# Queue places of the operand splits in the output stages of a two-layer encoder: tied to weight copies and additions in place of matmuls

## The chip, the cores and the metric

One core of a Trainium2 chip runs the whole program once. The metric is the device time of one execution in microseconds, the median of several runs. An execution takes a little longer than the span that its profile shows: the profiled one took 1505.1 us with a span of 1503.3 us.

## The reference

Two layers over a sequence of 1024 tokens of width 1024, float32. Layer 0 has global attention, windowed attention and attention into 256 memory tokens; layer 1 has neighbourhood attention on a grid and again memory attention. In both the concatenated heads are gated and go through one output projection that is added to the residual stream:

```python
y = jnp.concatenate([ya, yb, ym], axis=-1) * jax.nn.silu(gate)   # 1536 wide
x = x + y @ w_out_even[e]
...
y = jnp.concatenate([yc, ym], axis=-1) * jax.nn.silu(gate)       # 1536 wide
x = x + y @ w_out_odd[o]
...
return rmsnorm(x, final_norm_gain)
```

The change touches only how these two output projections are ordered on the engines.

## The kernel before

**Split numbers.** A float32 number is fed to TensorE as two parts of a shorter type (float32r): a high part, which is the rounded copy, and a low part, which is the number less its high part. ScalarE (ACT) makes the copy (`copy`, L124), VectorE (DVE) or GpSimd (POOL) the subtraction. A product of two split numbers is three matmuls: high weight by high operand, high by low, low by high. `split` (L126) does this for an operand: the copy on ACT, the subtraction on DVE (L128). `w_parts` (L1263) does it for a weight unit of 128x384: the copy `wh` on ACT, the remainder `wl` (L1267) on DVE and POOL by turns (`either`). Both have four buffers, and so has the raw unit `wraw`, which SyncE's DMA queue (SP) loads at L1312.

**An output stage** (`out_project`, L1297; layer 0 at about 650 to 779 us of the span, layer 1 at about 1380 to 1503 us) multiplies 1024 x 1536 by 1536 x 1024 in halves, by a scheme of seven half-sized products in place of eight. In the order of the code these are y11, t1, t2, t3, y22, y21 and t4, named by their operands. The operands t1 to t4 are sums and differences of blocks of y that were made and stored earlier, as were the weight sums s1 to s4. Each product has four PSUM banks (output tiles of 128x512), and each bank takes two weight units (`u` = 0, 1) of three contraction tiles: 2 x 3 x 3 = 18 matmuls of 512 columns. For y11, t3, y22, y21 and t4 (`product`, L1315) a bank is finished before the next. For t1 and t2 (`products`, L1324) the first units of all four banks come first and then the second units. When a bank is done, `plus` (L1345) adds it on DVE into one or two of the result tiles c11, c22, c12, c21, into which the residual was loaded, and `square` makes their squares on ACT for the norm that follows.

**The operands** are loaded by `y_parts` (L1209), six tiles a product, one DMA each on SP (L1223), and split by `split` on ACT and DVE. Their buffers alternate. In layer 0, y11, y22 and t4 use the tags q, q, k, k, va (`va` holds two tiles), t1 and y21 use q, q, k, k, v (`v` holds two), t2 and t3 use six tiles each of H. In layer 1 t4 uses H as well, and c11 and c22 do too. y11 is stored ready split and is only loaded. So the transfer of y22's operand can start as soon as y11's matmuls have let go of its tiles, which is long before y22 runs, and y21's as soon as t1's have.

**What sets the order.** The program goes through a planner that runs a simulated clock. It gives every engine, and SP, a fixed list of instructions in the order in which they would become ready by that clock, and among ready ones by a priority, which is the place in the code, moved forward by a number that `ahead(kind)` gives (L35: in the first output stage weights by 300, in the second additions by 150). On the chip each engine then works through its list in order, and an instruction that waits for a semaphore holds up all behind it on that engine. `issue_after(ins)` is a limit for the planner: what is traced inside the block and runs on the engine of `ins` is listed behind `ins`; it adds no wait. `behind_held` (L1202) does that for the last copy and subtraction of the attention before (`held`), in layer 1; in layer 0 `held` is empty.

**The ties before.** In `products`, `ends[u, i]` keeps the last matmul of each bank. `y_parts` takes one matmul as `after` and puts the splits in an `issue_after` block of it: t3's splits behind the first bank of t1, y22's behind the last bank of t2, y21's behind t3, t4's behind y22 (L1384, L1393, L1403, L1419). t2's and t1's last three splits are put off (`later`) and traced one after each first unit of a bank (L1338 to L1340), behind `held` alone.

Of the kernel before, what the change touches and what calls it, by code (L numbers as in the profile page):

```python
# [64 lines left out]
class Trunk:  # L65
# [1133 lines left out]
        return tiles  # L1199

    @contextmanager
    def behind_held(self):  # L1202

        with ExitStack() as held:
            for i in self.held:
                held.enter_context(self.tc.issue_after(i.ins))
            yield

    def y_parts(self, yd, tags, kind, after=None):  # L1209

        nc = self.nc
        parts, later = [], deque()
        for k, t in enumerate(self.halves(tags, F32R)):
            hi, lo = t[:, 0, :], t[:, 1, :]
            raw = lo.bitcast(F32)
            y1, y2 = yd[k], yd[6 + k]
            with self.ahead("y"):
                if kind == "y11":
                    nc.sync.dma_start(t.bitcast(F32), y1[:, 2:4, :])
                    parts.append((lo, hi))  # L1220
                    continue
                src = dict(t1=y1[:, 1, :], t2=y2[:, 3, :], t3=y2[:, 2, :], y22=y2[:, 0, :], y21=y2[:, 1, :], t4=y2[:, 4, :])
                nc.sync.dma_start(raw, src[kind])  # L1223
                if kind in ("t1", "t2") and k > 2:
                    later.append((hi, lo, raw))
                else:
                    with self.behind_held(), self.tc.issue_after(after.ins) if after else nullcontext():
                        self.split(hi, lo, raw)
                parts.append((hi, lo))
        return (parts, later) if kind in ("t1", "t2") else parts  # L1230
# [32 lines left out]
    def w_parts(self, raw, engine, n=3):  # L1263
        h, l = (self.st(t, [128, UNIT, 128], F32R, pool=self.base, bufs=4)[:, :n] for t in ("wh", "wl"))
        hf, lf = (t.rearrange("p a b -> p (a b)") for t in (h, l))
        self.copy(hf, raw)
        engine.tensor_tensor(lf, raw, hf, op=OP.subtract)  # L1267
        return h, l

# [27 lines left out]
    def out_project(self, w, sd, yd, res, done, tags, banks, first, begun, last=False):  # L1297
# [4 lines left out]
        nc = self.nc  # L1302
        xb, yb = banks
        cut = [slice(u * 384, u * 384 + 384) for u in range(2)]

        def weights(i, kind, us=(0, 1)):

            src = sd[i][:, "3124".index(kind[1]), :] if kind[0] == "s" else w[i if kind[1] == "1" else 4 + i][:, 768 * (kind[2] == "2"):]
            for c in (cut[u] for u in us):
                with self.ahead("w"):  # L1310
                    raw = self.st("wraw", [128, UNIT * 128], pool=self.base, bufs=4)[:, :384]
                    nc.sync.dma_start(raw, src[:, c])  # L1312
                    yield self.w_parts(raw, self.either())

        def product(y, bank, ws, start, cols=slice(0, 512), ks=range(6)):  # L1315
            for u, (h, l) in enumerate(ws):
                for k in (k for k in range(3) if 3 * u + k in ks):
                    for e, (s, m) in enumerate(((h, 0), (h, 1), (l, 0))):
                        last = nc.tensor.matmul(bank, s[:, k, :], y[3 * u + k][m][:, cols],  # L1319
                                                start=start and u + k + e == 0, stop=u == 1 and k + e == 4,  # L1320
                                                skip_group_check=True)
            return last

        def products(y, banks, kind, start, ready=()):  # L1324
            ready = deque(ready)
            y, later = y
            ends.clear()
            for u in range(2):
                for i, bank in enumerate(banks):
                    (h, l), = (ready.popleft(),) if ready else weights(i, kind, (u,))  # L1330
                    for k in range(3):
                        for e, (s, m) in enumerate(((h, 0), (h, 1), (l, 0))):
                            end = nc.tensor.matmul(bank, s[:, k, :], y[3 * u + k][m], start=start and u + k + e == 0,
                                                   stop=u == 1 and k + e == 4, skip_group_check=True)
                    ends[u, i] = end
                    if u:
                        yield i
                    elif later:  # L1338
                        with self.behind_held(), self.ahead("y"):
                            self.split(*later.popleft())  # L1340

        def residual(x, nt, half):
            nc.sync.dma_start(x, res[nt][:, 512 * (2 - half):512 * (3 - half)])

        def plus(x, p, op=OP.add):  # L1345
            nc.vector.tensor_tensor(x, x, p, op=op)

        def square(x, k):

            sq = self.st("ph" if k else "vt", [128, 512])  # L1350
            nc.scalar.activation(sq, x, AF.Square)
            if 0 < k < 7:
                nc.gpsimd.tensor_tensor(sums[0], sums[0], sq, op=OP.add)
            else:
                sums.append(sq)
        ends = {}
        c11, c22, c12, c21 = (self.halves(t) for t in tags["c"])
        at = lambda c, i: c[i // 2][:, i % 2, :]

# [1 line left out]
        for i in range(4):  # L1361
            if i >= begun:
                with self.tc.issue_after(self.hold.ins) if self.hold else nullcontext():
                    product(first, xb[i], weights(i, "a11") if i > begun else self.early, True)
            residual(at(c11, i), i, 1)
            with self.behind_held(), self.ahead("sink"):
                plus(at(c11, i), xb[i])

        ready = [w for i in range(2) for w in weights(i, "s1", (0,))]
        y = self.y_parts(yd, tags["y"][1], "t1")  # L1370
        for i in products(y, yb, "s1", True, ready):
            residual(at(c22, i), 4 + i, 2)
            with self.ahead("sink"):
                plus(at(c22, i), yb[i])

        after = [ends[1, 0]]
        y = self.y_parts(yd, tags["y"][2], "t2")
        for i in products(y, xb, "s2", False):
            residual(at(c12, i), i, 2)
            with self.ahead("sink"):  # L1380
                plus(at(c12, i), xb[i])

        sums = []
        y = self.y_parts(yd, tags["y"][3], "t3", after[0])  # L1384
        for i in range(4):
            end = product(y, xb[i], weights(i, "s3"), False)
            residual(at(c21, i), 4 + i, 1)
            with self.ahead("sink"):
                plus(at(c22, i), xb[i])
                plus(at(c21, i), xb[i])  # L1390
                square(at(c22, i), i)

        y = self.y_parts(yd, tags["y"][4], "y22", ends[1, 3])  # L1393
        for i in range(4):
            ending = product(y, yb[i], weights(i, "s4"), False)
            with self.ahead("sink"):
                plus(at(c12, i), yb[i])
                square(at(c12, i), 4 + i)
# [1 line left out]
        next(norm)  # L1400

        sums = []
        y = self.y_parts(yd, tags["y"][5], "y21", end)  # L1403
        fence = None
        for i in range(4):
            parts = list(weights(i, "a12"))
            with self.tc.issue_after(fence.ins) if fence else nullcontext():
                end = product(y, xb[i], parts, True)
# [5 lines left out]
            with self.ahead("sink"):  # L1414
                x = at(c11, i)
                plus(x, xb[i])
                square(x, i)

        y = self.y_parts(yd, tags["y"][6], "t4", ending)  # L1419
        for i in range(4):  # L1420
            x = at(c21, i)
            if last and i == 3:
# [763 lines left out]
```

## Time and profile before

| | |
|---|---|
| median of 3 runs | 1505.27 us (1504.47 to 1507.01) |
| the profiled execution | 1505.1 us, span 1503.3 us |
| TensorE busy (PE) | 1473.3 us, 98% of the span |
| VectorE (DVE) | 1032.9 us, 69% |
| ScalarE (ACT) | 841.2 us, 56% |
| GpSimd (POOL) | 636.2 us, 42% |
| DMA, mean over the span | 181 GB/s |

How to read the lines of the profile: in a list of groups or of the timeline, `L124 ACT ACTIVATE wh<-wraw` is line 124 of the kernel, the engine, the operation, and the tile written from the tile read; buffer numbers are left out. The timeline gives the start, the length and in brackets the engine's idle time before the instruction with what ended it; `x2` after the shape means that two alike were merged. A row of waits gives the engine and line that waited, what released it, the sum in us, the count and the longest. A row of DMA issues gives the count and, below it, the least, median and greatest time from issue to landing in us. PEld is TensorE's weight load, which overlaps its matmuls.

### The profile page before, as it was taken

The page shows a single profiled execution, that of the slowest core. Times are in us where ns is not written, and L with a number is a line of the kernel's source. Part 1 is how long each engine was busy: PE and PEld are TensorE (multiplying, and loading weights), DVE is VectorE, ACT ScalarE, POOL GpSimd, SP SyncE. Part 2 cuts the span into 40 slices and gives each one's busy share as a digit, 9 for nine tenths or more (in the row PEclk, how much of TensorE's full clock was granted, in tenths as well). Part 3 has the DMA queues.
Part 4 walks back from the last instruction along what each step waited for, and adds up shares of the span by engine and source line. Part 5 has one row for each costly group of instructions (what it writes and reads, how often), then busy time and mean ns, then how long its engine had stood idle before and what let it go on. Part 6 is the DMA issues. An engine that isn't in the chain of part 4 may idle for free.

```text
span 1503.3 us, 25289 instructions
## 1 busy us (share of the span) xinstructions
PE 1473.3 (98%) x8377; PEld 1266.8 (84%) x8377; DVE 1032.9 (69%) x2122; ACT 841.2 (56%) x1855; POOL 636.2 (42%) x762
## 2 busy tenths in 40 slices
PE   9999999999999999998999999999999999999997
PEld 8898888989888788786879877888988888888786
DVE  6786777677676677667577766654447778788744
ACT  7743665655655456554445444444447777777442
POOL 1223668556665655533450000002225556754355
PEclk9999999999999999999999999999999999999999
DMA  8966344433444423388653434558675677688833
GB/s 282 323 157 178 111 121 165 126 125 118 129 126 136 133 89 129 120 272 268 197 174 117 139 135 148 151 157 284 200 262 154 209 231 223 218 285 312 284 111 138
DMA packets 173859, 271.90 MB, mean 181 GB/s; under 512 B 15648, under 2 KB 96800, under 8 KB 172704
## 3 DMA queue, kind: packets, MB, share of 16 engines
q1 hardware_dynamic: 173296, 270.20, 56.0%
q8 instruction: 66, 1.08, 0.3%
q14 instruction: 65, 0.53, 0.1%
q10 hardware_dynamic: 432, 0.09, 0.0%
HBM read 174.28 MB, written 83.89 MB: 172 GB/s over the span
## 4 chain that ended last, share of the span: by engine, by line
PE 78%; DVE 7%; DMA 7%; issue 3%; ACT 2%; POOL 1%; SPq 1%; POOLq 0%; DVEq 0%; ACTq 0%
PE pj L241 15%; PE pj L62 10%; PE x L1585 6%; PE tr L132 5%; PE pv L1055 4%; PE y L1585 4%; PE pv L62 3%; PE pj L1319 3%; PE s L62 3%; PE sa L1319 2%; PE pv L1585 2%; PE tr L62 2%; PE s L1319 2%; PE sa L1022 2%; PE sa L1023 2%
## 5 line engine op out<-in xcount | busy, mean ns | idle before, releaser
L124 ACT ACTIVATE ph<-tr 128x512 fp32r<-128x512 f32 (+2 forms) x336 | 180.9, 540 | 118.3 <-PE tr L132 76.9
L537 DVE TENSOR_TENSOR pl<-tr,ph 128x512 fp32r<-128x512 f32 (+2 forms) x336 | 205.5, 615 | 54.0 <-ACT ph L124 52.9
L241 PE MATMUL pj<-H,wh 128*128 128x512 f32 x704 | 234.6, 413 | 0.5 <-DVE vt L312 0.2
L157 POOL TENSOR_SCALAR wh<-wraw 128x512 fp32r<-128x512 f32 x48 | 34.4, 719 | 268.3 <-PE x L1585 234.9
L124 ACT ACTIVATE wh<-wraw 128x384 fp32r<-128x384 f32 (+1 forms) x163 | 89.1, 553 | 89.9 <-PE pj L1319 12.0
L241 PE MATMUL pj<-H,wl 128*128 128x512 f32 x352 | 139.1, 395 | 0.0
L241 PEld LDWEIGHTS pj<-H,wh 128*128 128x128 f32 x704 | 120.0, 189 | 18.7 <-POOL wh L157 0.6
L62 PE MATMUL pj<-H,wh 128*128 128x512 f32 x384 | 121.5, 397 | 0.0
L1108 POOL TENSOR_SCALAR pn<-pn,st 128x384 f32<-128x384 f32 (+1 forms) x128 | 75.3, 589 | 99.6 <-DVE st L1107 58.0
L132 PE MATMUL tr<-ident,P 128*128 128x128 f32 x752 | 115.7, 273 | 0.9 <-DVE pl L537 0.6
L1267 POOL TENSOR_TENSOR wl<-wraw,wh 128x384 fp32r<-128x384 f32 x56 | 61.9, 1107 | 117.8 <-ACT wh L124 101.1
L132 PEld LDWEIGHTS tr<-ident,P 128*128 128x128 f32 x752 | 88.9, 140 | 9.6 <-DVE pl L537 1.7
L1028 ACT ACTIVATE P<-sa,st 128x1024 f32<-128x1024 f32 x64 | 71.5, 1118 | 41.5 <-DVE st L1027 22.7
L1106 ACT ACTIVATE pn<-pn,st 128x384 f32<-128x384 f32 (+1 forms) x128 | 75.1, 587 | 35.0 <-DVE st L1103 32.6
L62 PE MATMUL s<-k,q 128*128 128x384 f32 (+1 forms) x352 | 86.5, 342 | 0.1
L1030 POOL TENSOR_SCALAR P<-P,st 128x1024 f32<-128x1024 f32 x64 | 73.9, 1158 | 29.0 <-DVE st L1029 26.9
L1027 DVE TENSOR_REDUCE st<-sa 128x1 f32<-128x1024 f32 x64 | 77.6, 1218 | 10.9 <-PE sa L1023 10.5
L241 PEld LDWEIGHTS pj<-H,wl 128*128 128x128 f32 x352 | 66.2, 188 | 15.1
L62 PE MATMUL pj<-H,wl 128*128 128x512 f32 x192 | 75.8, 395 | 0.0
L159 POOL TENSOR_TENSOR wl<-wraw,wh 128x512 fp32r<-128x512 f32 x52 | 68.2, 1315 | 9.5 <-ACT wh L124 6.9
L62 PEld LDWEIGHTS pj<-H,wh 128*128 128x128 f32 x384 | 66.6, 189 | 5.5
L840 PE MATMUL pj<-ah,H 128*128 128x256 f32 x384 | 70.5, 282 | 0.2
(558 smaller groups left out, 4172.3 us busy)
## 6 DMA issues: line engine op xcount, KB each, us to landing
wraw<-w_o SPq DMA_DIRECT2D x52, 256.0 KB, 3.7
y<-yb SPq DMA_DIRECT2D x24, 512.0 KB, 3.6
wraw<-s SPq DMA_DIRECT2D x64, 192.0 KB, 3.4
wraw<-w_e SPq DMA_DIRECT2D x44, 256.0 KB, 3.2
k<-k SPq DMA_DIRECT2D x42, 256.0 KB, 4.8
s<-bias SPq DMA_DIRECT2D x56, 192.0 KB, 2.0
y<-sg SPq DMA_DIRECT2D x20, 512.0 KB, 3.6
wq<-w_o SPq DMA_DIRECT2D x40, 256.0 KB, 3.3
```

The source lines that it names most:

```text
L62: return lambda *a, **k: self.tc.keep_in_program_order(getattr(self.engine, name)(*a, **k))
L124: return self.nc.scalar.activation(out, in_, AF.Copy, scale=scale)
L132: self.turned = self.fence = self.pe.transpose(o, i, self.ident)
L241: self.pe.matmul(a[:, :n], s[:, kt % UNIT, :], m, start=(kt == 0 and i == 0), stop=(kt == KT - 1 and i == 2))
L537: self.low = nc.vector.tensor_tensor(pl[:, :n], tr[:, :n], ph[:, :n], op=OP.subtract)
L1027: nc.vector.tensor_reduce(st[:, 0:1], s, axis=AX.X, op=OP.max, negate=True)
L1028: nc.scalar.activation(pt, s, AF.Exp, bias=st[:, 0:1], accum_out=st[:, 1:2])
L1030: self.normal = nc.gpsimd.tensor_scalar(pt, pt, st[:, 2:3], 0.5, op0=OP.mult, op1=OP.mult)
L1106: nc.scalar.activation(o, o, AF.Exp, bias=st[:, 0:1], scale=-1.0, accum_out=st[:, 2:3])
L1108: normal = nc.gpsimd.tensor_scalar(o, o, st[:, 3:4], 0.5, op0=OP.mult, op1=OP.mult)
L1319: last = nc.tensor.matmul(bank, s[:, k, :], y[3 * u + k][m][:, cols], start=start and u + k + e == 0, stop=u == 1 and k + e == 4, skip_gro ...
L1585: self.last = nc.tensor.matmul(bank, ws[s][:, k, :], b[k][m], start=start and k + i == 0, stop=k == UNIT - 1 and i == 2, skip_group_check= ...
```

## The change

The ties are made to instructions of the two engines on which the splits run. `w_parts` keeps the last weight copy on ACT (`self.high`), `plus` the last addition on DVE (`self.added`), and `behind_held` takes more instructions to stand behind. `after` becomes such a pair: for t3 the pair in the middle of t1's second half, for y22 that at the end of t2, for y21 that at the end of t3, for t4 that at the end of y22. The put-off splits of t1 and t2 are listed behind the last weight copy on ACT. `ends` and the matmuls kept in `end` and `ending` for this go. No instruction with work is added or removed, and the loads of the operands (L1219, L1223) stand outside these blocks as before.

```diff
-    def behind_held(self):
+    def behind_held(self, more=()):
         with ExitStack() as held:
-            for i in self.held:
+            for i in (*self.held, *more):
                 held.enter_context(self.tc.issue_after(i.ins))
             yield
 
-    def y_parts(self, yd, tags, kind, after=None):
+    def y_parts(self, yd, tags, kind, after=()):
...
-                    with self.behind_held(), self.tc.issue_after(after.ins) if after else nullcontext():
+                    with self.behind_held(after):
                         self.split(hi, lo, raw)
...
     def w_parts(self, raw, engine, n=3):
...
-        self.copy(hf, raw)
+        self.high = self.copy(hf, raw)
...
         def products(y, banks, kind, start, ready=()):
...
-                    ends[u, i] = end
                     if u:
                         yield i
                     elif later:
-                        with self.behind_held(), self.ahead("y"):
+                        with self.behind_held((self.high,)), self.ahead("y"):
                             self.split(*later.popleft())
...
         def plus(x, p, op=OP.add):
-            nc.vector.tensor_tensor(x, x, p, op=op)
+            self.added = nc.vector.tensor_tensor(x, x, p, op=op)
...
         for i in products(y, yb, "s1", True, ready):
             residual(at(c22, i), 4 + i, 2)
             with self.ahead("sink"):
                 plus(at(c22, i), yb[i])
-
-        after = [ends[1, 0]]
+            if i == 1:
+                after = self.high, self.added
+
         y = self.y_parts(yd, tags["y"][2], "t2")
...
-        y = self.y_parts(yd, tags["y"][3], "t3", after[0])
+        y = self.y_parts(yd, tags["y"][3], "t3", after)
+        after = self.high, self.added
...
-        y = self.y_parts(yd, tags["y"][4], "y22", ends[1, 3])
+        y = self.y_parts(yd, tags["y"][4], "y22", after)
+        after = self.high, self.added
...
-        y = self.y_parts(yd, tags["y"][5], "y21", end)
+        y = self.y_parts(yd, tags["y"][5], "y21", after)
+        after = self.high, self.added
...
-        y = self.y_parts(yd, tags["y"][6], "t4", ending)
+        y = self.y_parts(yd, tags["y"][6], "t4", after)
```

More of the change, by code (lines that the diff above doesn't have):

```diff
@@ L1326, in products @@
             y, later = y
-            ends.clear()
             for u in range(2):
@@ L1332, in products @@
                         for e, (s, m) in enumerate(((h, 0), (h, 1), (l, 0))):
-                            end = nc.tensor.matmul(bank, s[:, k, :], y[3 * u + k][m], start=start and u + k + e == 0,
-                                                   stop=u == 1 and k + e == 4, skip_group_check=True)
-                    ends[u, i] = end
+                            nc.tensor.matmul(bank, s[:, k, :], y[3 * u + k][m], start=start and u + k + e == 0,
+                                             stop=u == 1 and k + e == 4, skip_group_check=True)
                     if u:
@@ L1355, in square @@
                 sums.append(sq)
-        ends = {}
         c11, c22, c12, c21 = (self.halves(t) for t in tags["c"])
@@ L1383, in out_project @@
         sums = []
-        y = self.y_parts(yd, tags["y"][3], "t3", after[0])
+        y = self.y_parts(yd, tags["y"][3], "t3", after)
+        after = self.high, self.added
         for i in range(4):
-            end = product(y, xb[i], weights(i, "s3"), False)
+            product(y, xb[i], weights(i, "s3"), False)
             residual(at(c21, i), 4 + i, 1)
@@ L1391, in out_project @@
                 square(at(c22, i), i)
-        y = self.y_parts(yd, tags["y"][4], "y22", ends[1, 3])
+        y = self.y_parts(yd, tags["y"][4], "y22", after)
+        after = self.high, self.added
         for i in range(4):
-            ending = product(y, yb[i], weights(i, "s4"), False)
+            product(y, yb[i], weights(i, "s4"), False)
             with self.ahead("sink"):
```

## The prediction

> **What bounds the kernel now.** I read first the page's table of engines, then busy time over the two output stages alone, then TensorE's waits in each stage, then the queues of ScalarE (ACT) and VectorE (DVE) around the waits that those named.
>
> ```profile
> PE 1473.3 (98%) x8377; PEld 1266.8 (84%) x8377; DVE 1032.9 (69%) x2122; ACT 841.2 (56%) x1855; POOL 636.2 (42%) x762
> ...
> 650.00:779.00 129.00, 124.97 (x561) 100.24 (x560) 86.84 (x135) 63.92 (x123) 58.03 (x50) 1.00 0.67 219
> 1380.00:1490.00 110.00, 107.53 (x482) 87.04 (x481) 66.41 (x101) 53.07 (x97) 54.01 (x46) 1.00 0.55 181
> ```
>
> The first row is the whole span: TensorE is busy for 98% of it. The other two are the stages (stretch, length, then busy us of PE, PEld, DVE, ACT, POOL, granted clock, DMA share, GB/s). The change adds and removes no matmul, copy, subtraction or transfer; it changes only which instruction stands ahead of which on ACT and DVE. So at first hand it can win only TensorE's idle time: 129.00 - 124.97 = 4.03 us in the first stage and 110.00 - 107.53 = 2.47 us in the second, 6.50 us together or 0.43% of the span. The clock is 1.00 in both, so nothing is to be won there. TensorE's waits name the pieces, first stage, then second:
>
> ```profile
> PE pj L1333 <- DVE wl L1267: 2.4, 1, 2.4
> PE tr L1333 <- DVE wl L1267: 1.0, 1, 1.0
> PE pj L1333 <- ACT wh L124: 0.4, 1, 0.4
> PE sa L1333 <- DVE P L1346: 0.2, 1, 0.2
> ...
> PE pj L1319 <- DVE wl L1267: 1.9, 1, 1.9
> PE tr L1333 <- POOL wl L1267: 0.3, 1, 0.3
> PE pj L1319 <- ACT wh L124: 0.2, 1, 0.2
> ```
>
> Six of the seven waits, 6.2 of 6.4 us, are for weights: the rounded copy `wh` or the remainder `wl`. Each weight unit goes through the queues that also carry the operand splits. So the question is what stands ahead of the late units. In the first stage, on ACT:
>
> ```profile
> 678.05 0.62 ACT L124 ACTIVATE va<-va 128x512 fp32r<-128x512 f32 x1
> ...
> 680.03 0.92 ACT L124 ACTIVATE wh<-wraw 128x384 fp32r<-128x384 f32 x2
> 686.04 0.63 ACT L124 ACTIVATE va<-va 128x512 fp32r<-128x512 f32 x1 [5.08 <-DMA va<-y]
> 687.21 0.63 ACT L124 ACTIVATE q<-q 128x512 fp32r<-128x512 f32 x1 [0.54 <-DMA q<-y]
> 688.54 0.63 ACT L124 ACTIVATE q<-q 128x512 fp32r<-128x512 f32 x1 [0.69 <-DMA q<-y]
> 689.07 0.92 ACT L124 ACTIVATE wh<-wraw 128x384 fp32r<-128x384 f32 x2
> ```
>
> The tile `va` belongs, after the first product, which needs no split, to y22 and then to t4. So both `va` splits here are y22's, and the two q behind them are y21's. In the code before, y22's splits stand in a block tied to the last matmul of t2. That product only starts here:
>
> ```profile
> 689.63 0.72 PE L1333 MATMUL pj<-H,wh 128*128 128x512 f32 x2 [0.36 <-ACT wh L124]
> 692.74 0.50 PE L1333 MATMUL pj<-H,wl 128*128 128x512 f32 x1 [2.38 <-DVE wl L1267]
> ```
>
> The splits run before even t2's first matmul. So the old tie holds nothing: a tie to a TensorE instruction orders nothing on ACT or DVE. Meanwhile the weight units that t2 needs first had landed (three issues, and how long they took to land):
>
> ```profile
> L1312 SPq DMA_DIRECT2D wraw<-s x3: 319/369/383, 681.4 to 683.8; - x3
> ...
> DMA to landing us min/median/max: 3.1/3.2/5.2
> ```
>
> The first was issued at 681.4 and landed 3.1 us later at 684.5, the second half a us behind it, the third, the slowest, at 683.8 + 5.2 = 689.0. But the first pair was copied at 689.07, because ACT stood for 5.08 us on the transfer of a `va` that is needed two products later, and then for two q. DVE then adds its share, with what POOL did meanwhile:
>
> ```profile
> 678.83 2.11 DVE L128 TENSOR_TENSOR k<-k 128x512 fp32r<-128x512 f32 x2
> 680.87 0.55 DVE L1267 TENSOR_TENSOR wl<-wraw,wh 128x384 fp32r<-128x384 f32 x1
> ...
> 687.87 1.71 DVE L128 TENSOR_TENSOR q<-q 128x512 fp32r<-128x512 f32 x1
> 689.51 0.67 DVE L1346 TENSOR_TENSOR P<-P,tr 128x512 f32<-128x512 f32 x1
> 690.11 1.51 DVE L128 TENSOR_TENSOR q<-q 128x512 fp32r<-128x512 f32 x1
> 691.54 0.68 DVE L1346 TENSOR_TENSOR P<-P,pv 128x512 f32<-128x512 f32 x1
> 692.14 0.54 DVE L1267 TENSOR_TENSOR wl<-wraw,wh 128x384 fp32r<-128x384 f32 x1
> 692.61 1.49 DVE L128 TENSOR_TENSOR k<-k 128x512 fp32r<-128x512 f32 x1
> 694.03 0.68 DVE L1346 TENSOR_TENSOR P<-P,sa 128x512 f32<-128x512 f32 x1
> ...
> 687.30 1.74 POOL L523 TENSOR_TENSOR yb<-sg,yb 128x512 f32<-128x512 f32 x1
> ```
>
> **The change, part by part.** *y22's and y21's splits* (six each per stage, on each engine) now queue behind the last weight copy and last addition of the product two ahead of their own use: y22's behind the end of t2, y21's behind the end of t3. They leave the stretch above. In the first stage the `wh` pair can then start at its landing, 684.5, instead of 689.07, and its `wl` follows about 0.5 us later, so both are there before TensorE ends t1 near 689: the 0.36 and 2.38 us go. The wait of 0.2 us is for the addition of 694.03, which stands behind the k split of 692.61 (1.49 us), also y21's: it goes. The wait of 1.0 us ended with the `wl` of 680.87, which stood behind two k splits of y22 (2.11 us): it goes too. Sum of the first stage: 0.36 + 2.38 + 0.2 + 1.0 = 3.94 us.
>
> What is late next there is a landing, not a queue: the third weight unit's transfer. The first two units last 2 x 2.09 us on TensorE (below), so with t2 starting at 689.0 the third is wanted at 693.2, 4.2 us after its landing at 689.0; its copy and remainder take under 2. So this costs 0.
>
> *The second stage.* The same ties move y22's and y21's splits out of t1 and t2, and t4's out of t3's stretch into y21's. The 0.3 us wait there is for a POOL remainder in t1, among y22's splits; ends 0 and 0.3, I take 0.3. The largest wait is another matter:
>
> ```profile
> 1419.49 0.52 ACT L124 ACTIVATE wh<-wraw 128x384 fp32r<-128x384 f32 x1
> ...
> 1418.96 1.88 DVE L128 TENSOR_TENSOR H<-H 128x512 fp32r<-128x512 f32 x3
> 1420.77 0.68 DVE L1346 TENSOR_TENSOR mk<-mk,pj 128x512 f32<-128x512 f32 x1
> 1421.37 1.28 DVE L1267 TENSOR_TENSOR wl<-wraw,wh 128x384 fp32r<-128x384 f32 x1
> ...
> L1312 SPq DMA_DIRECT2D wraw<-s x1: 319/319/319, 1414.1 to 1414.1; - x1
> ...
> DMA to landing us min/median/max: 5.3/5.3/5.3
> ```
>
> The first unit of t3 was issued at 1414.1, landed 5.3 us later at 1419.4 and was copied at 1419.49: ACT held it up by 0.1 us only. Its `wl` then waited for three H splits and an addition. Those H splits are t3's own, used next; their new tie (an addition and a weight copy in the middle of t1's second half) is one that they already stand behind. So I leave the 1.9 + 0.2 us where they are; the other end is that they go too.
>
> *t1's and t2's last three splits* are tied to a weight copy of the first half of their product and are used in its second half. At the least two units lie between, 2 x 2.09 = 4.2 us, against 0.6 + 0.7 us for a split: 0. *The new waits.* No semaphore is added, only a place in two queues. Queued behind a split that is not ready are weights and additions, as now; but a split placed one product ahead of its use finds its transfer landed long since, so it waits for nothing.
>
> *What the moved splits cost where they go.* They land in t3, y22 and y21, which run with no wait now. There TensorE's rhythm is seen in the additions:
>
> ```profile
> 1439.28 0.69 DVE L1346 TENSOR_TENSOR H<-H,s 128x512 f32<-128x512 f32 x1 [0.97 <-PE s L1319]
> 1443.47 0.69 DVE L1346 TENSOR_TENSOR mk<-mk,tr 128x512 f32<-128x512 f32 x1 [0.98 <-PE tr L1319]
> ...
> 708.60:727.00 18.40, 18.40 (x81) 14.89 (x80) 11.04 (x17) 7.40 (x15) 8.00 (x8) 1.00 0.44 135
> ```
>
> A product bank of two units takes 1443.47 - 1439.28 = 4.19 us, so a unit 2.09 us. With four buffers a unit can be prepared three units ahead, 6.3 us; less 0.5 us for its copy and about 1.1 for its remainder (0.55 to 1.28 above), 4.7 us of slack are left. Six splits in one block on DVE delay a remainder by 6 x 0.63 = 3.8 us undisturbed (the three H splits above took 1.88) and by 6 x 1.71 = 10.3 us if each met POOL as the q split of 687.87 did. In the stretch of t3 (last row) DVE is busy for 11.04 of 18.40 us, so the added 3.8 us fit. The bounds are 0 and 10.3 - 4.7 = 5.6 us for a block; I take 0, by the H splits, the nearer row, because DVE remainders alternate with POOL's and a block rarely stands whole before one.
>
> That 1.71 us split began while POOL's 1.74 us operation ran to 689.04 and ended 0.54 us after it. [...]
>
> Sum: 3.94 + 0.3 = 4.2 us won, ends 0 and 6.5. The profiled execution took 1505.1 us, 1.8 more than its span of 1503.3, and 0.2 less than the median of 1505.27. 1505.1 - 4.2 gives 1500.9; from the median it is 1501.1, which is my forecast. About 0.2%, 3 us, is what a measurement of this kernel can tell from no change (three runs spread by 2.5 us), so the forecast is just past it.
>
> **The rivals.** *No change, 1504.* The stall at t2 turns into another of like size: the H operands of t2's end and of t3 and the weights share the transfers, and with TensorE 3 us earlier they come 3 us too late, while the ties, being only a floor, leave it to the planner to put other splits ahead of the same `wl`. For it: the second stage's largest wait has just this form. Against it: in the first stage the late units had landed four us before they were copied. It leaves about 1 us of gain, 1504.
>
> *Slower, 1512.* In t3 of both stages y22's six splits stand as a block ahead of a remainder, each blocked by POOL: 5.6 us a block, 11.2 for two, less the 4.2 us won, so 1505.1 + 7.0 = 1512. It decides from the point where a split takes over 4.7 / 6 = 0.78 us on average. For it: four rows above show 1.05 to 1.71 us a split. Against it: those were in stretches where POOL's operations crowd, and the H splits took 0.63.
>
> *All waits go, 1499.* If splits that leave t2 also free t3's first unit, the 6.5 us go and it is 1498.6.
>
> **How the numbers follow.** Forecast (3 to 5.5 us won) 0.45; all waits go 0.12; no change 0.25; slower 0.18, most of it with smaller blocks than priced, at 1509 or below. Faster by over 0.2% is 0.45 + 0.12 = 0.57, within 0.2% 0.25, slower 0.18. The range runs from all idle time won, with the runs' spread of 0.8 us below their median, 1497.8, up over no change and into the smaller blocks, 1507.5; what is left out is half of the slower case and a little at the fast end. The likeliest case's own range is 1499.5 to 1502.3.
>
> **What would show it.** Right: in the first stage no ACT copy of `va` or q ahead of t2's first `wh`, that `wh` within half a us of its landing, TensorE idle under 1 us up to t3, and y22's splits inside t3's stretch. The second stage's wait at t3's first `wl` still there. Wrong: new waits of TensorE for `wl` or for q, k, v, va tiles in t3, y22 or y21; splits over 0.8 us there; or the same idle time at t2 with a transfer named as its releaser. A difference outside the two stages would mean that the planner's order changed elsewhere, which this sum does not hold.

## The result, and the profile after

| | before | after |
|---|---|---|
| median | 1507.01 us (1503.84 to 1513.15, 11 runs) | 1498.56 us (1496.94 to 1502.43, 11 runs) |
| ratio, 95% interval | | 0.994 (0.9927 to 0.9952) |
| profiled execution | 1505.1 us, span 1503.3 | 1502.43 us, span 1500.6 |

Faster by 0.6%: 8.45 us between the medians, 7.2 to 11.0 us by the interval. The prediction had 4.2 us and 1501.1 us; 1498.56 us lies inside its range and just below its likeliest case (1499.5 to 1502.3). Busy time of each engine over the whole span, from the page of after:

```profile
PE 1474.3 (98%) x8377; PEld 1268.5 (85%) x8377; DVE 1038.2 (69%) x2122; ACT 837.8 (56%) x1855; POOL 633.8 (42%) x762
```

The windows of its two output stages (stretch, length, then busy us of PE, PEld, DVE, ACT, POOL, granted clock, DMA share, GB/s):

```profile
650.00:779.00 129.00, 128.91 (x588) 104.97 (x587) 90.44 (x138) 67.27 (x129) 59.90 (x50) 1.00 0.70 234
1380.00:1490.00 110.00, 110.00 (x507) 90.03 (x506) 70.17 (x105) 51.92 (x99) 53.49 (x46) 1.00 0.56 184
```

TensorE's idle time is 0.09 us in the first stage (before 4.03) and 0.00 in the second (before 2.47). All seven waits of the prediction are gone, 6.4 us. The queues at t2 of the first stage, after: ACT, then DVE.

```profile
682.22 1.26 ACT L124 ACTIVATE v<-v 128x512 fp32r<-128x512 f32 x2 [2.85 <-DMA v<-y]
683.38 0.92 ACT L124 ACTIVATE wh<-wraw 128x384 fp32r<-128x384 f32 x2
686.24 0.53 ACT L124 ACTIVATE wh<-wraw 128x384 fp32r<-128x384 f32 x1 [1.93 <-PE tr L1332]
...
703.64 1.14 ACT L124 ACTIVATE q<-q 128x512 fp32r<-128x512 f32 x2
704.68 1.14 ACT L124 ACTIVATE k<-k 128x512 fp32r<-128x512 f32 x2
705.73 1.14 ACT L124 ACTIVATE va<-va 128x512 fp32r<-128x512 f32 x2
...
686.47 0.69 DVE L1344 TENSOR_TENSOR P<-P,tr 128x512 f32<-128x512 f32 x1 [1.79 <-PE tr L1332]
687.07 1.12 DVE L1267 TENSOR_TENSOR wl<-wraw,wh 128x384 fp32r<-128x384 f32 x1
688.12 0.68 DVE L1344 TENSOR_TENSOR P<-P,pv 128x512 f32<-128x512 f32 x1
...
710.39 1.51 DVE L128 TENSOR_TENSOR q<-q 128x512 fp32r<-128x512 f32 x2
711.83 1.28 DVE L128 TENSOR_TENSOR k<-k 128x512 fp32r<-128x512 f32 x2
713.03 1.28 DVE L128 TENSOR_TENSOR va<-va 128x512 fp32r<-128x512 f32 x2
```

y22's six splits, among them the two `va` copies that stood before at 678.05 and 686.04 us, now come as a block: the copies from 703.64 on, with no wait for a transfer, the subtractions from 710.39 on, behind t2's additions. They take 4.1 us for six, 0.68 a split. y21's six, whose q copies stood before at 687 to 689 us, follow one product later, the copies from 717.55 on. ACT's remaining wait (2.85 us for `v`) is for an operand of t1 itself. t2's first `wh` is the copy at 686.24; its unit was issued at 679.60 and landed 5.5 us later, so it was copied 1.2 us behind its landing and not within the half us that the prediction named as a sign. The row puts that wait down to TensorE (L1332), not to a split, and t2 starts only at 691.31, so it costs nothing.

The profiled execution of after is 3.9 us above its own median. In it TensorE lost about as much at 184 to 254 us, in a stretch whose instructions stand in the same order in both kernels. From the 4001st matmul on (665.57 us before, 669.46 after) to the last (1496.26 and 1493.58) the two profiles differ by 830.69 - 824.12 = 6.6 us. That is the 6.4 us of idle time and nothing else of note. What the medians show beyond it is taken up with the clock, in the part on the prediction.

### The profile page after: what moved, and what is told of

The parts are those of the page before. It is cut to its first block, busy times and chain, and to the rows that moved or that the text cites. A ratio compares the mean times of both kernels' runs of the same rounds, so it can differ in the third digit from the quotient of the medians.

```text
span 1500.6 us, 25250 instructions
## 1 busy us (share of the span) xinstructions
PE 1474.3 (98%) x8377; PEld 1268.5 (85%) x8377; DVE 1038.2 (69%) x2122; ACT 837.8 (56%) x1855; POOL 633.8 (42%) x762
## 4 chain that ended last, share of the span: by engine, by line
PE 79%; DMA 7%; DVE 6%; POOL 3%; issue 3%; ACT 2%; SPq 1%; POOLq 0%; DVEq 0%; ACTq 0%
PE pj L241 13%; PE pj L62 10%; PE x L1586 6%; PE tr L132 5%; PE y L1586 4%; PE pv L62 3%; PE pv L1055 3%; PE pj L1319 3%; PE sa L1319 3%; PE s L62 3%; PE tr L62 2%; PE pv L1586 2%; PE tr L1319 2%; PE s L1319 2%; PE pj L840 2%
```

## The experiments

All ratios are against the kernel before, run on the same chip in the same job.

**The old ties alone taken out** (`untied`):

```diff
-                    with self.behind_held(), self.tc.issue_after(after.ins) if after else nullcontext():
+                    with self.behind_held():
                         self.split(hi, lo, raw)
```

> The kernel before with the old matmul ties of the splits taken out. Theory that the old ties order nothing: the same program in the same order, so a ratio to the kernel before of 1.000 within its interval, and TensorE idle of 4.0 us at 650 to 779 us and of 2.5 us at 1380 to 1490 us again (give or take 1 us for landings that differ from run to run). Rival, that the old ties held something: slower, with splits of va or q earlier than before. The spread of this pair also tells how much of the 8 us between the medians of before and after can be run-to-run.

Measured: 0.9998 (0.9981 to 1.0014). The lists that the planner gives the five engines' queues are the same to the last instruction with and without the old ties. So they ordered nothing, and this is a second sample of the kernel before. Its idle time is again 129.00 - 124.71 = 4.29 us and 110.00 - 107.67 = 2.33 us. But its stages' granted clock is not 1.00: it is 0.99 and 0.98. Busy time in 5 us stretches, the third column from the end being the granted clock; the first pair stands at t2 of the first stage, the second at t3 of the second:

```profile
690.00:695.00 5.00, 2.55 (x9) 1.53 (x9) 5.00 (x7) 1.90 (x5) 2.01 (x2) 0.96 0.55 178
695.00:700.00 5.00, 5.00 (x16) 3.83 (x16) 3.65 (x7) 2.72 (x5) 0.16 (x1) 0.70 0.99 307
1420.00:1425.00 5.00, 3.02 (x12) 1.89 (x11) 5.00 (x9) 3.67 (x8) 1.00 (x1) 1.00 0.92 346
1425.00:1430.00 5.00, 5.00 (x17) 3.92 (x16) 4.29 (x7) 2.28 (x5) 1.01 (x1) 0.66 0.92 296
```

In the first stretch of each pair TensorE stands idle for 2.45 and 1.98 us, and within the next 5 us the clock is low: (1 - 0.66) x 5 = 1.7 us are lost, and 16 or 17 matmuls run where 23 do in a full stretch. Such a stretch of low clock is called a dip below.

**The program of before once more** (`untied2`, no edit beside the one above):

> The program of the kernel before once more, for one more profile of it. In the profile of before the clock was 1.00 throughout the stages, in that of the untied kernel it fell to 0.5 for 3.4 us behind t2's stall and behind t3's. Theory that a stall of 2 to 3 us sets off a clock dip in some executions and not in others: the same stalls of 2.4 and 1.9 us, and either a dip within 10 us behind one of them or none, but no dip elsewhere in the two stages. Rival (dips fall anywhere): dips away from any idle time.

Measured: 1505.74 us in the one run; the same wait of 2.4 us at t2, one of 1.5 us at t3 of the second stage, two of 0.4 and 0.8 us late in the first stage, and the clock at 1.00 in both stages. So a stall may or may not be followed by a dip. Over all profiles with t2's full stall (before, `untied`, `untied2`, `second_stage`) a dip stands behind it in 2 of 4; with one in t3 of the second stage (before, `untied`, `untied2`, `first_stage`, 1.6 us in `y21`, and 2.3 us some 10 us into t3 in `y22`) in 2 of 6. The other dips in the two stages are behind new stalls, in `act_tie` and `late` below. None stands in a stage without idle time.

**Only y22's and y21's ties** (`y22_y21`), and **everything but these** (`rest`):

```diff
 y22_y21:
-                        with self.behind_held((self.high,)), self.ahead("y"):
+                        with self.behind_held(), self.ahead("y"):
-        y = self.y_parts(yd, tags["y"][3], "t3", after)
+        y = self.y_parts(yd, tags["y"][3], "t3")
-        y = self.y_parts(yd, tags["y"][6], "t4", after)
+        y = self.y_parts(yd, tags["y"][6], "t4")
 rest:
-        y = self.y_parts(yd, tags["y"][4], "y22", after)
+        y = self.y_parts(yd, tags["y"][4], "y22")
-        y = self.y_parts(yd, tags["y"][5], "y21", after)
+        y = self.y_parts(yd, tags["y"][5], "y21")
```

> Of the change, only the ties of y22's and y21's splits. Queue theory (those splits, waiting on transfers ahead of weight copies, are the cost): nearly all of the gain, TensorE idle under 1 us in each output stage, 6 us or 0.4% faster than before. Rival (the put-off splits of t1 and t2, or t4's tie, carry it): idle in the stages stays over 4 us together and the gain is under 2 us.

> The complement: the change without the ties of y22's and y21's splits; t1's, t2's put-off splits, t3's and t4's ties stay. Queue theory: the va copy of the first stage again waits about 5 us ahead of t2's first weight copies, idle there about 3 us, gain at most 2 us. Rival (the put-off splits carry it): idle under 1 us in each stage and a gain of 5 us or more.

`y22_y21` measured 0.9938 (0.9919 to 0.9956), the whole of the change, with a single wait of 0.4 us on the norm's rows at the end of the first stage and none before 1490 us of the second but the norm's own 1.9. `rest` measured 0.9955 (0.9937 to 0.9973), 5.7 us between the medians: by its gain it meets the rival's sign of 5 us or more, by its idle time in the first stage the queue theory's of about 3 us. Its waits, first stage:

```profile
PE tr L1332 <- DVE v L128: 1.0, 1, 1.0
PE pv L1332 <- ACT k L124: 0.7, 1, 0.7
PE sa L1332 <- DVE P L1344: 0.6, 1, 0.6
PE tr L1332 <- DVE wl L1267: 0.4, 1, 0.4
PE pj L1332 <- DVE wl L1267: 0.2, 1, 0.2
```

2.9 us stay in the first stage, in five short pieces; in the second only 0.15. ACT again stands for 4.61 us on a transfer, of a q tile, ahead of t2's first weight copy, as expected, but the waits at t2 are only 0.2 and 0.6 us. So y22's and y21's ties are enough for all of the gain, but they are not the only way to it: the other ties alone mend the second stage and shorten t2's stall. The two parts overlap and do not add up.

**Only y21's tie** (`y21`) and **only y22's** (`y22`), each as `y22_y21` with the other's `after` taken out:

```diff
 y21, beside the edits of y22_y21:
-        y = self.y_parts(yd, tags["y"][4], "y22", after)
+        y = self.y_parts(yd, tags["y"][4], "y22")
 y22, beside the edits of y22_y21:
-        y = self.y_parts(yd, tags["y"][5], "y21", after)
+        y = self.y_parts(yd, tags["y"][5], "y21")
```

> Of the change, only the tie of y21's splits. Theory of VectorE's queue (what ScalarE's tie alone and VectorE's tie alone left standing): in the first stage the wait of 2.4 us at t2 goes, since the q and k splits of 1.5 to 1.7 us ahead of its remainder are y21's; the wait of 1.0 us at t1 stays, behind y22's k splits; ScalarE still waits 4 to 5 us on va, and TensorE does not. Theory of ScalarE's wait on va: t2's stall stays at 2 us or more.

> Of the change, only the tie of y22's splits. Theory of VectorE's queue: the wait of 1.0 us at t1 goes; y21's splits still stand ahead of t2's remainders, idle of 1 us or more at t2. Theory of ScalarE's wait on va: t2's stall goes and the stage's idle is under 1 us.

Measured: 0.9969 (0.9956 to 0.9982) and 0.997 (0.9959 to 0.9982), each about half. ACT and DVE at t2 of the first stage in `y21`, from the timeline:

```profile
690.22 0.64 ACT L124 ACTIVATE va<-va 128x512 fp32r<-128x512 f32 x1 [4.71 <-DMA va<-y]
690.76 0.92 ACT L124 ACTIVATE wh<-wraw 128x384 fp32r<-128x384 f32 x2
...
691.50 0.68 DVE L1344 TENSOR_TENSOR P<-P,tr 128x512 f32<-128x512 f32 x1
692.09 0.77 DVE L1267 TENSOR_TENSOR wl<-wraw,wh 128x384 fp32r<-128x384 f32 x1
```

TensorE's waits in that stage of `y21` (total, number, longest, in us):

```profile
PE tr L1332 <- DVE wl L1267: 1.0, 1, 1.0
PE pv L1332 <- DVE yb L743: 0.7, 1, 0.7
PE sa L1332 <- POOL wl L1267: 0.5, 1, 0.5
```

ACT stands for 4.71 us on `va` ahead of t2's first two weight copies, just as before, and TensorE does not wait at t2: the three rows are all of t1. So the long wait on `va` alone makes no stall. What this run takes away from t2 are y21's two q copies between `va` and the weight copies, and their subtractions of 1.71 and 1.51 us ahead of `wl`. The 1.0 us at t1, behind y22's k splits, stays as expected. In `y22`, where y21's splits stay, the waits at t1 and t2 for `wl` go as well, and one of 1.3 us comes at t2, for an addition behind y21's splits:

```profile
PE sa L1332 <- DVE P L1344: 1.3, 1, 1.3
```

So y22's tie alone takes t2's waits from 0.36 + 2.38 + 0.21 = 2.95 us to 1.3, and y21's alone to nothing: y21's splits are the larger part of the stall at t2, not all of it. The second stage of `y22` keeps 2.3 us.

**ScalarE's tie alone** (`act_tie`) and **VectorE's alone** (`dve_tie`):

```diff
-            for i in (*self.held, *more):
+            for i in (*self.held, *more[:1]):     # dve_tie: *more[1:]
```

> The change with the ties kept on ScalarE alone (the additions on VectorE are left out of the pair). Theory that the wait on ScalarE, for a transfer ahead of weight copies, starts the stall: a subtraction can't run before its copy, so this does nearly what the whole change does; TensorE idle under 1 us in each output stage, as fast as the change within 2 us. Rival (VectorE's queue is what delays the weights): idle of 2 us or more comes back at t2.

> The change with the ties kept on VectorE alone; the copies on ScalarE are free, and the put-off splits of t1 and t2 too. Theory of the wait on ScalarE: copies of y22's va and y21's q stand again ahead of t2's first weight copies, idle of 2 to 3 us at t2 of the first stage, gain 2 to 4 us smaller than the change's. Rival (VectorE's queue): under 1 us of idle in each stage, as fast as the change.

Measured: `act_tie` 0.9976 (0.9961 to 0.9992), `dve_tie` 0.9947 (0.9929 to 0.9966): the reverse of what I expected. TensorE's waits in `act_tie`, first stage:

```profile
PE sa L1319 <- DVE P L1344: 2.0, 1, 2.0
PE pj L1319 <- ACT wh L124: 1.0, 1, 1.0
```

ACT at t2 of the same stage in `dve_tie`, from the timeline:

```profile
690.48 0.63 ACT L124 ACTIVATE va<-va 128x512 fp32r<-128x512 f32 x1 [3.73 <-DMA va<-y]
691.01 0.51 ACT L124 ACTIVATE wh<-wraw 128x384 fp32r<-128x384 f32 x1
```

Neither has the stall at t2, so these two don't tell there what the copies and what the subtractions cost. With only ACT tied, y22's subtractions get in front of t2's last additions on DVE, and at t3 TensorE waits 2.0 us for a bank that such an addition has to read first. With only DVE tied, ACT still waits 3.73 us on `va`, and TensorE has 0.7 us of idle time in the whole stage. So the tie on VectorE is enough, and the one on ScalarE is not. At the end of `act_tie`'s two waits stands a dip of twice the usual length, (1 - 0.52) x 5 + (1 - 0.80) x 5 = 3.4 us lost:

```profile
710.00:715.00 5.00, 4.14 (x9) 2.88 (x10) 3.66 (x7) 0.00 (x0) 0.98 (x1) 0.52 0.38 118
715.00:720.00 5.00, 5.00 (x19) 3.94 (x19) 1.84 (x3) 1.93 (x4) 1.01 (x1) 0.80 0.27 90
```

**One product later** (`late`): y22, y21 and t4 behind the end of the product just ahead of their own.

```diff
-        y = self.y_parts(yd, tags["y"][4], "y22", after)
-        after = self.high, self.added
+        y = self.y_parts(yd, tags["y"][4], "y22", (self.high, self.added))
```

and the same for y21 and t4.

> The change with the ties of y22, y21 and t4 one product later: behind the last weight copy and the last addition of the product just ahead of their own. Theory that the slack of a whole product is what makes the change free: TensorE waits at each of these six product starts (three in either stage) for an addition of 0.7 us, a copy of 0.6 and a subtraction of 0.7, about 2 us each, 12 us idle in all and 1511 us or more. Rival (any place behind the weights does): no new waits for q, k, v or va, as fast as the change. Second question: whether a granted clock of 0.5 for some microseconds follows idle stretches of TensorE of 2 to 3 us, as the profile of the untied kernel shows twice: then dips stand behind some of these starts, and the time is up to 1.7 us longer for each; without the link the clock stays at 1.00.

Measured: 1.009 (1.0062 to 1.0119), 1521.25 us. The windows of its two stages:

```profile
650.00:779.00 129.00, 119.09 (x525) 95.53 (x524) 83.63 (x131) 61.24 (x118) 55.00 (x47) 0.96 0.64 212
1380.00:1490.00 110.00, 102.95 (x457) 81.77 (x455) 69.21 (x105) 53.94 (x106) 48.03 (x43) 1.00 0.59 196
```

TensorE's waits in the first stage:

```profile
PE pj L1319 <- DVE q L128: 8.0, 2, 6.7
PE tr L1319 <- DVE q L128: 1.6, 1, 1.6
PE pj L1319 <- DVE P L1344: 0.3, 1, 0.3
```

9.9 and 7.05 us idle (1.8 of the second the norm's own), against 12 expected in all. Five of the six starts cost 1.3 to 2.2 us, as worked out; t4's of the first stage costs 6.7, since its splits then stand on DVE, busy for all of 760 to 770 us, behind the norm's operations, and the clock falls during that wait: the 0.96 is (1 - 0.96) x 129 = 5.2 us lost. On the second question: a dip stands at t4's start in both stages (the second one at 1492, outside the window above), and none at the other four. One product of slack is what makes the splits free.

**One stage alone** (`first_stage`, `second_stage`): `behind_held` uses `more` only in the output stage of layer 0, or of layer 1 (`self.last_stage` is set to `last` at the head of `out_project`).

```diff
 first_stage:
-            for i in (*self.held, *more):
+            for i in (*self.held, *(() if self.last_stage else more)):
 second_stage:
-            for i in (*self.held, *more):
+            for i in (*self.held, *(more if self.last_stage else ())):
```

> The change in the output stage of layer 0 alone; the second stage is untied. Theory that the two stages add up, each its own idle time plus the clock dips that the idle time sets off: idle under 0.5 us at 650 to 779 us, about 2.5 us again in the second stage with the waits at t1 (0.3) and t3 (1.9); 0.3 to 0.4% faster than before, more than half of the change's 0.6%. Rival (the gain is of the whole plan, shifted by the planner): no such split.

> The change in the output stage of layer 1 alone. The same theory: idle of about 4.0 us again in the first stage with the waits of 1.0, 0.4 and 2.4 us, none from 1380 to 1490 us; 0.1 to 0.3% faster than before.

Measured: 0.9972 (0.9959 to 0.9984) and 0.9973 (0.9962 to 0.9984). Together 0.55%, which is the change's 0.6% within the intervals. The idle time is where it was expected: 0.48 and 3.07 us in `first_stage`, 4.72 and 0.16 in `second_stage`. Both show a dip behind the stall that was left. t3's of the second stage in `first_stage`, in windows of 5 us:

```profile
1413.00:1418.00 5.00, 2.72 (x11) 1.58 (x10) 5.00 (x9) 3.65 (x7) 1.00 (x1) 1.00 0.89 324
1418.00:1423.00 5.00, 5.00 (x17) 3.92 (x16) 4.67 (x7) 2.55 (x5) 1.01 (x1) 0.66 0.83 273
```

t2's of the first stage in `second_stage`:

```profile
690.00:695.00 5.00, 3.14 (x14) 1.98 (x12) 4.38 (x6) 3.62 (x7) 3.51 (x3) 1.00 0.87 319
695.00:700.00 5.00, 4.44 (x12) 3.53 (x13) 3.57 (x7) 1.57 (x3) 1.05 (x1) 0.66 0.73 238
```

No version measured beats the change beyond its interval, and the change leaves 0.09 us of idle time in the stages.

## Why the prediction was right, and where its steps failed

**That the old ties held nothing: shown.** `untied` has the same queues.

**The first stage, 3.94 us: right in size, wrong on the main cause.** The waits went, 4.0 us. But I put the stall at t2 down to ACT's 5.08 us on `va` and gave DVE "its share". `y21` and `dve_tie` keep a wait of 4.71 and 3.73 us on `va` and lose the stall. The larger part is y21's splits, whose tie alone leaves no wait at t2, while y22's alone leaves 1.3 us. How much of it their copies and how much their subtractions make is argued and not shown: in the rows of before the 1.51 us subtraction and an addition stand right ahead of the late `wl` at 692.14.

**The second stage, 0.3 us: the term that was mis-sized.** It measured 2.4 us. I left t3's 2.1 us where they were, because ACT copied the unit 0.1 us after it landed. That landing was itself a consequence: the load was issued late. SP works through its list in order. Its issue of t3's H tiles in the kernel before and the first load for t3 behind them, from the timeline:

```profile
1409.06 4.14 SPq L1223 DMA_DIRECT2D H<-y  x6
1414.06 0.32 SPq L1312 DMA_DIRECT2D wraw<-s  x1
```

Three of these six after, and below the dots the first load for t3:

```profile
1402.24 1.38 SPq L1223 DMA_DIRECT2D H<-y  x3
...
1409.42 2.38 SPq L1312 DMA_DIRECT2D wraw<-s  x2
```

The load now issues at 1409.42 instead of 1414.06, while t3's first matmul moved only from 1420.07 to 1419.58. Before, it did not wait for its buffer, which is free when the copy and remainder of the unit four before are done; it stood behind the six H loads, 4.14 us long. The last such remainder, before and after:

```profile
1407.20 0.77 DVE L1267 TENSOR_TENSOR wl<-wraw,wh 128x384 fp32r<-128x384 f32 x1
...
1408.82 0.55 DVE L1267 TENSOR_TENSOR wl<-wraw,wh 128x384 fp32r<-128x384 f32 x1
```

The H loads in turn stand on SP's list behind the stores of the last block of operands (L495, L498), and there SP waited 3.0 and 1.3 us for GpSimd, which makes them from the last gated block of y. That block's last multiplication runs on VectorE among the splits. Before and after:

```profile
1392.09 1.50 DVE L475 TENSOR_TENSOR yb<-yb,mk 128x512 f32<-128x512 f32 x1
...
1385.73 0.68 DVE L475 TENSOR_TENSOR yb<-yb,mk 128x512 f32<-128x512 f32 x1
```

From here to the H loads each link comes earlier by 6.4 to 8.1 us: the multiplication, the read-back (1393.99, after 1386.82), GpSimd's first operation on it (1400.09 and 1392.67), the last store (1404.88 and 1396.82), t3's first H load (1409.06 and 1401.29). The planner also gives SP a somewhat different list, so this chain is read from the two traces and not shown by a run of its own. All runs agree with it: where t3's first unit has no stall, its load issues 9.55 to 10.40 us ahead of t3's first matmul (after, `y22_y21`, `rest`, `act_tie`, `dve_tie`, `late`, `second_stage`), 8.86 us with a wait of 0.2 us (`y22`), and 5.75 to 6.32 us where it has the stall (before, `untied`, `untied2`, `y21`, `first_stage`). A landing just ahead of its use is no proof that the transfer was the limit; one has to ask what its issue waited for. The wait at t3's first `wl`, which the prediction expected to stay, is gone; its rival "all waits go" had this at 0.12. That its 1498.6 us meets the measured 1498.56 is luck: the median of before moved up by 1.7 us, from 1505.27 to 1507.01, and the clock, which it left out, won about as much.

**The clock: a step that failed.** "Nothing is to be won there" rested on one profile in which no dip happened. Dips stood behind these two stalls in 2 of 4 and 2 of 6 profiles; at 1.7 us each that is 0.5 x 1.7 + 0.33 x 1.7 = 1.4 us on average, an estimate. With the 6.4 us of idle time it makes 7.8 us, inside the measured 7.2 to 11.0. The record also has the mean granted clock of each execution. It is 0.9976 on average over the 11 of after, and 0.9964, 0.9962 and 0.9960 over the 20, 19 and 24 of before in the three jobs of the experiments (the 11 of before in the table have none on record). A difference of 0.0012 to 0.0016 of 1500 us is 1.8 to 2.4 us, an estimate too; with 6.4 us it makes 8.2 to 8.8, against 8.45 measured. So the clock accounts for the rest in size. That all of it comes from dips behind these stalls isn't shown, since dips also stand elsewhere.

**What the moved splits cost: 0 as taken, though not by the reason given.** There is no new wait in t3, y22 or y21. y22's splits took 0.68 us, under the 0.78 from which the slower rival decides, but y21's in the first stage took longer:

```profile
726.75 2.38 DVE L128 TENSOR_TENSOR q<-q 128x512 fp32r<-128x512 f32 x2
729.05 1.28 DVE L128 TENSOR_TENSOR k<-k 128x512 fp32r<-128x512 f32 x2
730.25 2.10 DVE L128 TENSOR_TENSOR v<-v 128x512 fp32r<-128x512 f32 x2
```

That is 5.6 us for six, 0.93 a split, over both the 0.78 and the 0.8 that the prediction named as a sign of being wrong, and still TensorE did not wait. So the slack was more than the 4.7 us of the sum; by how much no run shows. In two of the three pairs stands a split that met POOL:

```profile
727.03 1.54 POOL L1351 TENSOR_TENSOR vt<-vt,ph 128x512 f32<-128x512 f32 x1 [0.39 <-ACT ph L1349]
727.35 1.78 DVE L128 TENSOR_TENSOR q<-q 128x512 fp32r<-128x512 f32 x1
...
730.74 1.07 POOL L1267 TENSOR_TENSOR wl<-wraw,wh 128x384 fp32r<-128x384 f32 x1 [2.16 <-ACT wh L124]
730.86 1.50 DVE L128 TENSOR_TENSOR v<-v 128x512 fp32r<-128x512 f32 x1
```

Both ended 0.55 us behind the POOL operation, as the 1.71 us split of the prediction did (0.54). It is so in before's profile too: of its 72 splits on DVE from 640 us on, 14 took over 0.8 us, and each of these began while a POOL operation ran and ended 0.55 us behind it. The others took 0.68 to 0.78 us, among them three, from 1384.68 us on, beside one POOL operation of 2.78 us. POOL was busy there for 8.00 of 18.40 us in t3's stretch and for 9.17 of 17.00 us in the one behind it (727 to 744 us), where y21's splits now stand. The rival's mechanism is real: `act_tie` and `late` show what a block of splits in the wrong place costs, waits of 2.0 and 6.7 us. The no-change rival fell with the idle time at 0.09 us.

## What to carry to other kernels

On engines that work through a list in order, place work that is ready early by its use, not by its readiness: a whole product ahead was free here, behind the end of the product just ahead it was 13 us slower than the kernel before (1521.25 against 1508.07 us), and listed by readiness, up to two products ahead, it had cost 8. A planner's order limit has to name an instruction of the engine on which the work runs; a limit that names another engine's may silently hold nothing (`untied`: 0.9998), and comparing the lists shows it. Price a TensorE stall at more than its idle time: behind 4 of the 10 stalls counted above the clock took another 1.7 us.

## What the runs showed of the hardware

In after's profile TensorE's clock fell to half for 3.4 us behind a single wait of 1.2 us, in code that the change does not touch. The wait:

```profile
PE tr L132 <- POOL P L650: 1.2, 1, 1.2
```

The windows around it, and below the dots some of 0.5 us, the third column from the end being the granted clock:

```profile
223.00:228.00 5.00, 3.40 (x15) 2.10 (x14) 2.96 (x6) 1.49 (x3) 4.92 (x8) 1.00 0.37 112
228.00:233.00 5.00, 5.00 (x17) 3.90 (x16) 1.66 (x2) 1.12 (x2) 4.92 (x5) 0.66 0.35 111
...
227.50:228.00 0.50, 0.38 (x3) 0.29 (x3) 0.00 (x0) 0.00 (x0) 0.50 (x2) 1.00 0.87 276
228.00:228.50 0.50, 0.50 (x3) 0.40 (x2) 0.00 (x0) 0.36 (x1) 0.50 (x1) 0.50 1.00 274
...
230.50:231.00 0.50, 0.50 (x3) 0.40 (x2) 0.00 (x0) 0.00 (x0) 0.50 (x2) 0.50 0.00 0
231.00:231.50 0.50, 0.50 (x2) 0.39 (x2) 0.00 (x0) 0.00 (x0) 0.50 (x1) 0.58 0.00 0
231.50:232.00 0.50, 0.50 (x4) 0.38 (x3) 0.00 (x0) 0.00 (x0) 0.50 (x2) 1.00 0.40 102
```

The clock is 0.50 in all six windows from 228.00 to 231.00, so (1 - 0.50) x 3.0 + (1 - 0.58) x 0.5 = 1.7 us are lost. Behind stalls of 1.9 to 2.4 us in the output stages (`untied`, `first_stage`, `second_stage`) windows of 5 us show the same 1.7 us, in some executions and not in others of one program. At `act_tie`'s 2.0 us 3.4 us were lost, with the clock at 0.52 over a window of 5 us, and in `late`'s wait of 6.7 us 5.1 us, with 0.53, 0.50 and 0.95 over the three windows of 5 us from 765 us on. At half clock that is 6.8 and about 10 us of low clock, an estimate from these windows: twice and three times as long.

The same wait stands in six of the 13 profiles. It is followed by a dip where it is 0.9, 1.2, 1.3 and 1.4 us (`y21`, after, `dve_tie`, `y22`), and not where it is 0.6 and 0.8 us (`y22_y21`, `untied2`). At about 35 us it is alike: waits of 1.7 and 1.8 us in four profiles are each followed by a dip, and none of the other profiles, whose waits there are 0.9 us at most, has one. So in these two places the length of the wait went with the dip, while in the output stages equal stalls did not always bring one.

All the dips but the one in `late`'s wait of 6.7 us followed gaps of 0.9 to 2.4 us. Why the same stall is followed by a dip in one execution and not in the next, no run here shows.
